# Gate weights split to high and low parts in the first feed-forward, longer reckoned loads, and two token blocks per bank for the sparse queries

## The chip, the cores and the metric

The kernel runs on one core of one Trainium2 chip. The metric is the device time of one execution in microseconds, taken as the median of several runs. The engines are named in the profile as PE (TensorE, matrix products), PEld (its weight loads), DVE (VectorE), ACT (ScalarE), POOL (GpSimd) and SP (SyncE, which issues every DMA here).

## What is computed

One layer on 1024 tokens of width 1024: a first SwiGLU feed-forward (inner width 2816), a mixer, and a second feed-forward, each behind an RMS norm that is scaled and shifted by a conditioning vector. The mixer is what the change is about:

```python
z = h @ w_in
(fq, fk, fv, ff, dq, dk, dv, iq, ik, iw, ga, gb) = jnp.split(z, split_points, axis=-1)
...
ya = fox_attention(fq, fk, fv, log_f).reshape(B, S, FOX_WIDTH)
...
yb = dsa_attention(dq, dk, dv, iq, ik, iw, top_k).reshape(B, S, DSA_WIDTH)
merged = jax.nn.sigmoid(ga) * (ya @ w_br_fox) + jax.nn.sigmoid(gb) * (yb @ w_br_dsa)
return merged @ w_out
```

`ga` and `gb` are the gates, 1024 columns each, so 2048 columns of `w_in`. `dq` are the queries of the sparse attention, 8 heads of 64. The sparse attention keeps for each query the 256 keys with the highest index score, for which the kernel searches a threshold per query.

## The kernel before, in words

**Arithmetic.** Every large product runs as three matmuls (`mm3`, line 457): an operand is held as a high part rounded to the matmul's type and a low part that is the rest, and high x high, high x low and low x high are summed in PSUM. A weight that comes from DRAM is therefore split on the chip: `load_w` (line 565) loads 128x1024 raw values, ScalarE copies them to the high part `wh`, GpSimd subtracts to get the low part `wl`.

**Order of the work.** From line 205 on, the class `Plan` collects the instructions of a stage and puts them into an order for each engine's queue, on a model: `length` (line 302) reckons each instruction, and `flush` (line 322) always places the one that can start first, in rank order among equals. A step marked with `behind = n` gets a rank n instructions later. A DMA on SyncE is reckoned in line 395: it goes over one wire of 345 GB/s that begins 1.3 us after its issue, and its data counts as there 0.7 us after that. GpSimd and VectorE instructions that only touch SBUF are not placed at the same time. What the chip then does in the queues is in that order, at its own pace. A stage's instructions all stand ahead of the next stage's in each queue.

**First feed-forward (to about 690 us).** Eleven pairs of inner blocks go through `up_all` (line 1603), which counts its steps in `k.up_step`, 130 in all: ten for each of the first six pairs, whose first four steps are done before, and fourteen for each of the other five. One step is a product of 12 matmuls. A table `steps` calls further work at given steps; conditioning vectors of later layers are worked in by `extra`. Then `Down` (line 1643) does the second projection. Tiles of 128x512 come from a common pool of 52 (`t512`, line 576), and split weights from 8 pairs of halves.

**The gates' stage (to about 1049 us).** The function `layer` (line 1942) builds one list `g1` (lines 2232 to 2235): the third and fourth group of fox projections, two groups of sparse queries (`dq_group`, line 1026), and between them the 16 gate blocks of the first 512 tokens (`gates`, line 1072). One gate block is 24 matmuls of 512 columns, a tanh on ScalarE and a store of the tile `gt`. Beside it `topk` (line 839) searches the thresholds bit by bit: for three of six query blocks ScalarE counts with Sign (`tks`), for the other three VectorE counts (`tkj`), and small VectorE steps (`tkv`, `tku`, `tkkey`, `tkca`, `tkcand`) set the next bit; at the end `thr` is written. Weights come through `Ahead` (line 1054), which holds three loaded and split blocks ahead, from a ring of five pairs of tiles (`Ring`, line 546).

A group of queries or fox projections in its wide form (`group`, line 963) runs over eight blocks of 128 tokens at once, each in a PSUM bank of its own, taken from `chain8` (line 62): four banks as halves of the two tiles `p2` and four banks `pj`, the same that the gates use. Query blocks are 256 columns, a half bank. When a block is done, ScalarE copies it to the tile `qkv` (`norm_group`, line 1001).

**Attention (to about 1398 us).** Fox attention over four pairs of heads, then sparse attention over four, woven with the masks and the 16 gate blocks of the second 512 tokens (`gates` with PSUM name `py`). Only two split weight blocks are kept here, one ahead. GpSimd scales the probabilities. Then come the branches, the output product and the second feed-forward.

The functions follow, with the line numbers of the profile (all instructions carry L425, the line that issues planned instructions, so tiles tell them apart).

Of the kernel before, what the change touches and what calls it, by code (L numbers as in the profile page):

```python
# [21 lines left out]
D = 1024  # L22
# [3 lines left out]
H = 512  # L26
# [35 lines left out]
def chain8(one, two):  # L62

    while True:
        for _ in range(2):
            t = two()
            yield t[:, 0:H]
            yield t[:, H:T]
        for _ in range(4):
            yield one()  # L70


class Pairs:
# [131 lines left out]
class Plan:  # L205
# [116 lines left out]
    def flush(self, keep=()):  # L322
# [42 lines left out]
        while len(order) < len(tasks):  # L365
# [26 lines left out]
            free[e] = s + d  # L392
            if e == "sync":
                self.wire = max(self.wire, s + 1.3) + t.bytes / 345e3
                end = self.wire + 0.7
                free[e] = max(free[e], self.wire - 5.0)
            t.placed = True
            if t.group:
# [147 lines left out]
class Ring:  # L546
# [12 lines left out]
    def pair(self):  # L559
        p, n = self.split[self.i % len(self.split)]  # L560
        self.i += 1
        return tuple(p.tile([128, D], F32R, tag=t, name=t, bufs=n) for t in ("wh", "wl"))


def load_w(k, src, n):

    nc = k.nc
    raw = k.w.raw()
    nc.sync.dma_start(raw[:, :n], src)
    hi, lo = k.w.pair()  # L570
    nc.scalar.activation(hi[:, :n], raw[:, :n], AF.Copy)
    k.lo_eng.tensor_sub(lo[:, :n], raw[:, :n], hi[:, :n].bitcast(F32))
    return hi, lo
# [389 lines left out]
def group(k, src, n, ptile, wide, done, weight=1.9):  # L963


    if not wide:
        w = load_group(k, src, n)
        for tk in range(8):
            ps = ptile()
            proj_n(k, ps[:, :n], w, n, tk)  # L970
            done(tk, ps)
            tick(k)
            yield
        return
    ps = []
    for i in range(4):
        hi, lo = next(src)
        for tk in range(8):
            if i == 0:
                ps.append(ptile())  # L980
            hf, o = tk // 4, (tk % 4) * 128
            for c in range(2):
                hh, hl = (t[hf][2 * i + c][:, o:o + 128] for t in (k.hh, k.hl))
                cs = slice(c * n, c * n + n)
                mm3(k, ps[tk][:, :n], hh, hl, hi[:, cs], lo[:, cs], i + c == 0, i == 3 and c == 1)
            if i == 3:
                done(tk, ps[tk])
            if tk % 2:
                tick(k)
                yield weight  # L990
# [10 lines left out]
def norm_group(k, p, tmp, src, n, ptile, wide, weight=1.9):  # L1001

    t = [p.tile([128, 4, n], F32, tag="qkv", name="qkv", bufs=3) for _ in range(2)]
    v = tmp.tile([128, 8, 4], F32, tag="fv", name="fv", bufs=2)

    def done(tk, ps):
        k.nc.scalar.activation(t[tk // 4][:, tk % 4, :], ps[:, :n], AF.Copy)
        if tk % 2:
            later(k, 1, lambda: squares(k, tmp, v, t, tk))

    yield from group(k, src, n, ptile, wide, done, weight)
    r = head_factor(k, 32, v.rearrange("p a b -> p (a b)"), tmp, "fn").rearrange("p (a b) -> p a b", a=8)
    for h in range(2):
        x = t[h][:, :, 0:256].rearrange("p a (h d) -> p a h d", h=4)
        k.nc.vector.tensor_mul(x, x, r[:, 4 * h:4 * h + 4, :, None].to_broadcast([128, 4, 4, 64]))
    return t
# [925 lines left out]
def layer(tc, xT, c, pos, ada_w, ada_b, ng, inv, w13a, w2a, w_a, w_f, w_q, w_g, fb, fg, dg, wbr, wout, w13b, w2b, out):  # L1942
    with ExitStack() as es:
# [35 lines left out]
        k.pz_i = 0  # L1979
        k.tails, k.now = [], 0  # L1980
        k.lo_eng = nc.gpsimd
        dram = lambda shape, nm: dp.tile(shape, F32, name=nm)
        d_x = dram([8, 128, T], "d_x")
        d_row = [[dram([1, H], f"d_row{i}{h}") for h in range(2)] for i in range(9)]
        k.d_na = dram([8, 128, NA], "d_na")
# [13 lines left out]
        with ExitStack() as ph:  # L1999
# [24 lines left out]
            def consts():  # L2024
                yield
                nc.vector.tensor_copy(k.ident_r, k.ident)
                nc.vector.tensor_copy(k.ident_b, k.ident)
                cm = t512(k, name="cm")[:, 0:128]
                nc.gpsimd.memset(cm, 0.0)
                nc.gpsimd.affine_select(cm, cm, pattern=[[-1, 128]], compare_op=ALU.is_ge, fill=BIG, base=0,  # L2030
                                        channel_multiplier=1)
                nc.vector.tensor_copy(k.causal_b, cm)
                yield
                nc.vector.tensor_scalar(k.g_dq, k.g_dq, -0.125, None, op0=ALU.mult)
                k.g_fk = g2[:, 1:2]
                nc.vector.tensor_scalar(g2[:, 0:1], g2[:, 0:1], -0.125, None, op0=ALU.mult)
                k.g_fq = g2[:, 0:1]
                yield
                rope_tables(k, pos_i, t512(k, name="rt"), it)
                yield  # L2040

            sq1 = [SquareSum(k, nc.vector), SquareSum(k, nc.vector)]
            wa = []
# [76 lines left out]
            for i in range(2, head):  # L2120
# [3 lines left out]
                if i == 4:  # L2124
# [9 lines left out]
            pos_i = k.c.tile([128, 8], I32, name="pos_i")  # L2134
            nc.sync.dma_start(pos_i, pos)
            more()
            rest = up_all(k, pairs, head, [], {2: [more], 4: [more], 6: [more]}, lambda: down.loads(down.LEAD), chain(consts(), rest),
                          (nc.vector, nc.vector), True, lambda n: n % 2)
            steps = {(5, 4): [lambda: stats(0)]}
            steps.update({(6, c): [lambda c=c: h0(range(c, c + 2))] for c in range(0, 8, 2)})  # L2140
            steps.update({(5, c): steps.get((5, c), []) + [lambda c=c: load_wa(c - 1)] for c in range(1, 9)})
# [4 lines left out]

            for q in range(4 * PAIRS):
                steps.setdefault(divmod(q, PAIRS), []).append(more_mod)
            down.run(steps)
            assert next(rest, None) is None  # L2150
            nc.flush([t for r in down.x for t in r] + [t for r in wa for t in r] + k.hh[0] + k.hl[0] + [a.acc for a in sq1])
            w0s.close()
            w1 = pool(s1, "w1", True, side="right")
# [48 lines left out]
        with ExitStack() as ph:  # L2202
# [14 lines left out]

            parts = []
            for i, (w, n) in enumerate(((w_f[2], 768), (w_f[3], 768), (w_q[0], 512), (w_q[1], 512))):
                parts += [(w[j], n, r5) for j in range(4)] + [(w_g[b], D, r5) for b in range(3 * i, 3 * i + 3)]  # L2220
            ws = Ahead(k, parts + [(w_g[b], D, r5) for b in range(12, 16)] + [(w_g[b], D, r2) for b in range(2)], 3)
            nc.flush(k.hh[0] + k.hl[0] + k.hh[1] + k.hl[1] + [t for w in ws.q for t in w])
        k.ap0 = pool(s3, "att0", True)
        ps = ExitStack()
# [2 lines left out]
        with ExitStack() as ph:  # L2227
            tp = pool(ph, "topk", True)
            pj = lambda: pq.tile([128, H], F32, tag="pj", name="pj", bufs=4)
            bank8 = chain8(pj, p2)  # L2230
            gt = gates(k, ws, 0, tp, pj, 2)
            g1 = chain(fox_group(k, fp, fp, ws, 2, lambda: next(bank8), True), islice(gt, 15),
                       fox_group(k, fp, fp, ws, 3, lambda: next(bank8), True), islice(gt, 15),
                       dq_group(k, fp, fp, tp, ws, 0, lambda: next(bank8), 0.8), islice(gt, 15),
                       dq_group(k, fp, fp, tp, ws, 1, lambda: next(bank8), 0.6), gt)
            beside(behind(nc, topk(k, tp), 100), 66, at(g1, fox_qk(k, 0, None, lambda dt: pj()), (110, 122, 128, 134, 138)), 135.0)
            nc.flush(k.hh[1] + k.hl[1] + k.q2 + k.k2 + [t for w in ws.q for t in w])
        ws.parts, ws.n = [(w_g[b], D, r2) for b in range(2, 16)] + [(wbr[b], D, r2) for b in range(2)], 1
        fox.close()
        s1.close()  # L2240

# [168 lines left out]
```

## Time and profile before

| what | value |
|---|---|
| median of 3 runs | 2230.95 us (2229.25 to 2231.05) |
| profiled execution, its own time | 2230.78 us |
| span of the profiled execution, first to last instruction | 2229.0 us |
| mean granted clock of TensorE | 0.994 |
| TensorE busy | 2166.7 us, 97% |
| VectorE, ScalarE, GpSimd busy | 1638.6, 1145.2, 252.0 us |
| DMA traffic | 315.88 MB, 142 GB/s over the span |

Busy time of an engine is the union of its instructions. Matmuls are pipelined, so a busy TensorE is not one that issues at its peak. An idle time is written behind the instruction that ended it, with the instruction that it waited for. The clock is the share of TensorE's full rate that was granted.

### The profile page before, as it was taken

How to read it: one execution, taken by the hardware profiler on the slowest of the kernel's cores; microseconds unless marked ns; L12 is line 12 of the kernel's file. 1: busy time of each engine (PE TensorE's matmuls, PEld its weight loads, DVE VectorE, ACT ScalarE, POOL GpSimd, SP SyncE). 2: the span in 40 equal slices, each digit the busy share in tenths (PEclk: the TensorE clock that was granted, in tenths of full speed). 3: DMA queues.
4: the chain of work that ended last, by engine and by line, in shares of the span. 5: the costliest groups of instructions: out<-in, count | busy, mean ns of one | idle time of the engine just before them, and what ended most of it. 6: DMA issues, size and time to landing. Idle time of an engine off the chain costs nothing.

```text
span 2229.0 us, 31185 instructions
## 1 busy us (share of the span) xinstructions
PE 2166.7 (97%) x10700; PEld 1782.9 (80%) x10700; DVE 1638.6 (74%) x3095; ACT 1145.2 (51%) x2105; POOL 252.0 (11%) x225
## 2 busy tenths in 40 slices
PE   7999999999999999989999998999999999999999
PEld 5877788887889899977777777777778888888887
DVE  7968776688684698888887677498865755558665
ACT  5634433444464566787777677244443333334443
POOL 0000000000010222223445343000000000000000
PEclk9999999999999999999999999999999999999999
DMA  9245543695421323235232212596224443258520
GB/s 333 95 149 178 173 152 109 213 351 195 125 89 57 109 78 130 96 123 161 90 120 88 72 39 81 202 354 189 66 81 132 137 130 103 96 207 287 166 76 38
DMA packets 186267, 315.88 MB, mean 142 GB/s; under 512 B 27238, under 2 KB 51814, under 8 KB 186108
## 3 DMA queue, kind: packets, MB, share of 16 engines
q1 hardware_dynamic: 186108, 313.89, 42.4%
q8 instruction: 84, 1.38, 0.3%
q14 instruction: 75, 0.61, 0.1%
HBM read 237.53 MB, written 76.28 MB: 141 GB/s over the span
## 4 chain that ended last, share of the span: by engine, by line
PE 82%; DVE 8%; ACT 5%; DMA 3%; issue 2%; SPq 0%; POOL 0%; DVEq 0%; ACTq 0%; POOLq 0%
PE bs L425 34%; PE b L425 28%; PE py L425 7%; PE pj L425 6%; PE p L425 5%; PE pt L425 2%; DVE qkv L425 1%; ACT tks L425 1%; DVE xc L425 1%; DMA mraw<-in_ada_w 1%; DMA wr<-in_w_f 1%; ACT pth L425 1%; ACT pr L425 1%; ACT wh L425 1%; DVE wl L425 1%
## 5 line engine op out<-in xcount | busy, mean ns | idle before, releaser
L425 PE MATMUL bs<-h,wh 128*128 128x512 f32 x1728 | 543.0, 395 | 1.6 <-ACT bs L425 1.3
L425 ACT ACTIVATE wh<-wr 128x512 fp32r<-128x512 f32 (+2 forms) x366 | 246.5, 679 | 451.7 <-PE bs L425 208.3
L425 PEld LDWEIGHTS bs<-h,wh 128*128 128x128 f32 x1728 | 322.9, 188 | 81.9 <-ACT bs L425 5.7
L425 PE MATMUL b<-h,wh 128*128 128x512 f32 x1088 | 344.8, 397 | 5.7 <-ACT z L425 2.6
L425 PE MATMUL bs<-h,wl 128*128 128x512 f32 x864 | 338.7, 393 | 0.5 <-DVE wl L425 0.5
L425 DVE TENSOR_TENSOR wl<-wr,wh 128x512 fp32r<-128x512 f32 x308 | 205.4, 686 | 123.5 <-ACT wh L425 116.6
L425 PEld LDWEIGHTS b<-h,wh 128*128 128x128 f32 x1088 | 205.0, 189 | 55.5 <-ACT z L425 3.5
L425 PE MATMUL b<-h,wl 128*128 128x512 f32 x544 | 214.7, 395 | 0.1
L425 PEld LDWEIGHTS bs<-h,wl 128*128 128x128 f32 x864 | 162.2, 188 | 39.2 <-DVE wl L425 0.9
L425 ACT ACTIVATE wh<-a 128x512 fp32r<-128x512 f32 x132 | 83.3, 631 | 174.4 <-PE b L425 93.0
L425 POOL TENSOR_TENSOR wl<-wr,wh 128x1024 fp32r<-128x1024 f32 (+2 forms) x58 | 123.8, 2137 | 328.6 <-ACT wh L425 323.3
L425 DVE TENSOR_TENSOR wl<-a,wh 128x512 fp32r<-128x512 f32 x132 | 91.3, 692 | 88.1 <-ACT wh L425 83.5
L425 PE MATMUL b<-wh 128*128 128x512 f32 x352 | 137.2, 390 | 0.7 <-ACT mrow L425 0.7
L425 PE MATMUL b<-wh,wl 128*128 128x512 f32 x352 | 137.0, 389 | 0.0
L425 PE MATMUL b<-wl,wh 128*128 128x512 f32 x352 | 137.0, 389 | 0.0
L425 PE MATMUL pj<-wh,h 128*128 128x384 f32 (+1 forms) x512 | 125.8, 324 | 0.3 <-ACT wh L425 0.2
L425 PEld LDWEIGHTS b<-h,wl 128*128 128x128 f32 x544 | 102.8, 189 | 25.1 <-DVE wl L425 0.7
L425 DVE TENSOR_TENSOR z<-bs,z 128x512 f32<-128x512 f32 x116 | 79.3, 687 | 58.7 <-PE bs L425 36.8
L425 POOL TENSOR_SCALAR pr<-pr,mn 128x128 f32<-128x128 f32 (+7 forms) x128 | 100.0, 801 | 134.7 <-DVE mn L425 127.5
L425 DVE TENSOR_TENSOR wl<-g,wh 128x512 fp32r<-128x512 f32 x154 | 106.5, 694 | 2.5 <-ACT wh L425 2.5
L425 ACT ACTIVATE pr<-pr,mn 128x256 f32<-128x256 f32 (+7 forms) x128 | 98.4, 770 | 18.0 <-DVE mn L425 17.7
L425 PE MATMUL bs<-wl,wh 128*128 128x512 f32 x264 | 103.1, 391 | 2.1 <-DVE wl L425 1.9
(322 smaller groups left out, 4405.2 us busy)
## 6 DMA issues: line engine op xcount, KB each, us to landing
d_g<-z SPq DMA_DIRECT2D x154, 256.0 KB, 2.1
g<-d_g SPq DMA_DIRECT2D x154, 256.0 KB, 4.7
mraw<-in_ada_w SPq DMA_DIRECT2D x144, 256.0 KB, 5.3
wr<-in_w13a SPq DMA_DIRECT2D x112, 256.0 KB, 5.3
wr<-in_w13b SPq DMA_DIRECT2D x88, 256.0 KB, 4.6
wr<-in_w_g SPq DMA_DIRECT2D x32, 512.0 KB, 4.2
a<-in_w2a SPq DMA_DIRECT2D x44, 256.0 KB, 5.1
a<-in_w2b SPq DMA_DIRECT2D x44, 256.0 KB, 5.3
```

The costliest lines, as they stand in the source:

```text
L425: getattr(getattr(self.tc.nc, e), t.op)(*map(real, t.a), **{n: real(v) for n, v in t.kw.items()})
```

## The change

The weights of the 16 gate blocks are split once, during the first feed-forward, into DRAM tensors `d_wg` of high and low parts; 64 calls of a generator, from step 30 to step 124, do two halves of 512 columns per block (a load, a ScalarE copy, a GpSimd subtraction, then two stores), ranked 200 instructions behind. Both later passes over the gates load the parts straight into the tiles `wh` and `wl`, two DMAs of 512 KB in place of a load, a copy and a subtraction. Split tiles of the ring are handed out in order. The plan reckons that a DMA's data is there 1.0 us later than before. In the groups of sparse queries two token blocks of 256 columns share a bank, so that a group takes the four half tiles of `p2` alone and one ScalarE copy empties two blocks; the fox groups (384 columns) keep one block per bank.

```diff
@@ Plan.flush @@
-                end = self.wire + 0.7
+                end = self.wire + 1.7
@@ Ring.pair @@
-        return tuple(p.tile([128, D], F32R, tag=t, name=t, bufs=n) for t in ("wh", "wl"))
+        return tuple(p.tile([128, D], F32R, tag=t, name=t, bufs=n, in_turn=True) for t in ("wh", "wl"))
@@ load_w @@
+    if isinstance(src, tuple):
+        t = k.w.pair()
+        for part, d in zip(t, src):
+            nc.sync.dma_start(part[:, :n].bitcast(F32), d)
+        return t
@@ group, wide @@
-    ps = []
+    ps, m = [], H // n
...
-            if i == 0:
+            if i == 0 and tk % m == 0:
                 ps.append(ptile())
...
-                mm3(k, ps[tk][:, :n], hh, hl, hi[:, cs], lo[:, cs], i + c == 0, i == 3 and c == 1)
-            if i == 3:
-                done(tk, ps[tk])
+                mm3(k, ps[tk // m][:, tk % m * n:tk % m * n + n], hh, hl, hi[:, cs], lo[:, cs], i + c == 0,
+                    i == 3 and c == 1, tk % m > 0)
+            if i == 3 and tk % m == m - 1:
+                done(tk, ps[tk // m])
@@ norm_group @@
-        k.nc.scalar.activation(t[tk // 4][:, tk % 4, :], ps[:, :n], AF.Copy)
+        m = H // n if wide else 1
+        k.nc.scalar.activation(t[tk // 4][:, tk % 4 - m + 1:tk % 4 + 1, :], ps[:, :m * n].rearrange("p (a b) -> p a b", a=m),
+                               AF.Copy)
@@ layer @@
+        d_wg = split_in(16, D, "wg")
...
+        todo = [(w[i], d[i]) for w, d in (((w_g, d_wg),)) for i in range(len(d))]
...
+            def parts():
+
+                for src, dst in todo:
+                    n = dst[0].shape[1]
+                    m = n if n <= H else n // 2
+                    for c in range(0, n, m):
+                        nc.behind = 200
+                        t, hi, lo = (t512(k, dt, "gw")[:, :m] for dt in (F32, F32R, F32R))
+                        nc.sync.dma_start(t, src[:, c:c + m])
+                        nc.scalar.activation(hi, t, AF.Copy)
+                        nc.gpsimd.tensor_sub(lo, t, hi.bitcast(F32))
+                        nc.behind = 0
+                        yield
+                        nc.behind = 200
+                        for d, x in zip(dst, (hi, lo)):
+                            nc.sync.dma_start(d[:, c:c + m], x.bitcast(F32))
+                        nc.behind = 0
+                        yield
...
+            gw = parts()
+            steps = {2: [more], 4: [more], 6: [more]}
+            for n in range(64):
+                steps.setdefault(30 + 96 * n // 64, []).append(lambda: next(gw, None))
...
-                parts += [(w[j], n, r5) for j in range(4)] + [(w_g[b], D, r5) for b in range(3 * i, 3 * i + 3)]
-            ws = Ahead(k, parts + [(w_g[b], D, r5) for b in range(12, 16)] + [(w_g[b], D, r2) for b in range(2)], 3)
+                parts += [(w[j], n, r5) for j in range(4)] + [(d_wg[b], D, r5) for b in range(3 * i, 3 * i + 3)]
+            ws = Ahead(k, parts + [(d_wg[b], D, r5) for b in range(12, 16)] + [(d_wg[b], D, r2) for b in range(2)], 3)
...
-                       dq_group(k, fp, fp, tp, ws, 0, lambda: next(bank8), 0.8), islice(gt, 15),
-                       dq_group(k, fp, fp, tp, ws, 1, lambda: next(bank8), 0.6), gt)
+                       dq_group(k, fp, fp, tp, ws, 0, lambda: next(bank4), 0.8), islice(gt, 15),
+                       dq_group(k, fp, fp, tp, ws, 1, lambda: next(bank4), 0.6), gt)
...
-        ws.parts, ws.n = [(w_g[b], D, r2) for b in range(2, 16)] + [(wbr[b], D, r2) for b in range(2)], 1
+        ws.parts, ws.n = [(d_wg[b], D, r2) for b in range(2, 16)] + [(wbr[b], D, r2) for b in range(2)], 1
```

`chain4` yields the two halves of `p2` tiles in turn. Smaller lines without effect on the work (empty loops, unused tensors) are left out.

## Rows read from the trace of the kernel before

**Rows 1.** The page, part 1: busy us of each engine.
```profile
PE 2166.7 (97%) x10700; PEld 1782.9 (80%) x10700; DVE 1638.6 (74%) x3095; ACT 1145.2 (51%) x2105; POOL 252.0 (11%) x225
```

**Rows 2.** Stretches: length; busy us of PE, PEld, DVE, ACT, POOL; clock, DMA, GB/s.
```profile
192.00:457.00 265.00, 264.71 (x1139) 212.25 (x1139) 188.38 (x299) 102.29 (x177) 0.00 (x0) 1.00 0.54 179
457.00:506.00 49.00, 48.32 (x213) 39.27 (x212) 43.57 (x72) 23.95 (x43) 0.00 (x0) 1.00 0.99 356
```

**Rows 3.** The same columns: the gates' stage, and the attention.
```profile
843.00:1049.00 206.00, 197.08 (x1102) 175.37 (x1100) 170.05 (x505) 161.66 (x297) 58.67 (x30) 0.98 0.39 124
1049.00:1398.00 349.00, 332.77 (x2302) 266.06 (x2303) 269.14 (x599) 250.93 (x548) 149.41 (x155) 0.98 0.27 85
```

**Rows 4.** The same columns, in stretches of 50 us.
```profile
600.00:650.00 50.00, 50.00 (x226) 41.52 (x225) 34.28 (x59) 26.80 (x49) 10.95 (x8) 1.00 0.27 85
...
950.00:1000.00 50.00, 45.43 (x274) 40.90 (x275) 42.84 (x128) 41.11 (x80) 13.68 (x8) 0.93 0.42 132
```

**Rows 5.** Timeline of PE: start us, us, instruction, idle before.
```profile
1037.79 0.39 PE L425 MATMUL pj<-h,wl 128*128 128x512 f32 x1
...
1049.16 1.06 PE L425 MATMUL pt<-ident,nat 128*128 128x128 f32 x8 [1.29 <-DMA nat<-d_qkv]
```

**Rows 6.** Timeline of DVE at the end of the threshold search.
```profile
1042.10 0.17 DVE L425 TENSOR_SCALAR tkca<-tkkey 128x3 f32<-128x3 f32 x1
...
1046.06 0.17 DVE L425 SCALAR_TENSOR_TENSOR tkkey<-tkv,tkkey 128x3 f32<-128x3 f32 x1
...
1049.21 0.16 DVE L425 TENSOR_TENSOR thr<-tkku,tkm 128x3 uint32<-128x3 uint32 x1
```

**Rows 7.** The tile tks: ns min/median/max, first and last start us.
```profile
L425 ACT ACTIVATE tks<-tkh,tkca x51: 921/1042/1159, 843.5 to 948.9; 128x1024 bf16<-128x1024 uint16 x17, 128x896 bf16<-128x896 uint16 x17, 128x768 bf16<-128x768 uint16 x17
...
L425 ACT ACTIVATION_READ_ACCUMULATOR tks<-tkl,tkca x48: 185/188/240, 953.5 to 1045.6; 128x1 f32 x48
```

**Rows 8.** Groups by form, 843 to 1049 us: busy us, mean ns, idle before.
```profile
L425 POOL TENSOR_TENSOR wl<-wr,wh 128x1024 fp32r<-128x1024 f32 x16 | 38.5, 2404 | 95.0 <-ACT wh L425 95.0
L425 POOL TENSOR_TENSOR wl<-wr,wh 128x512 fp32r<-128x512 f32 x8 | 10.3, 1292 | 45.3 <-ACT wh L425 45.3
...
L425 ACT ACTIVATE wh<-wr 128x1024 fp32r<-128x1024 f32 x16 | 16.9, 1054 | 10.9 <-issue 10.9
```

**Rows 9.** Groups by form of DVE, 843 to 1049 us.
```profile
L425 DVE TENSOR_TENSOR qkv<-qkv,fnr 128x1024 f32<-128x1024 f32 x9 | 14.9, 1690 | 0.1
L425 DVE TENSOR_TENSOR tku<-tkcnt,tklim 128x3 uint32<-128x3 f32 x32 | 11.7, 365 | 0.8
L425 DVE TENSOR_TENSOR tkv<-tksgn,tklim 128x3 f32<-128x3 f32 x32 | 11.4, 355 | 23.4 <-ACT tks L425 23.2
...
L425 DVE SCALAR_TENSOR_TENSOR tkkey<-tkv,tkkey 128x3 f32<-128x3 f32 x32 | 5.2, 162 | 1.1
L425 DVE TENSOR_TENSOR qkv<-qkv,g_dq 128x1024 f32<-128x1024 f32 x4 | 4.9, 1216 | 0.0
```

**Rows 10.** Timeline of PE around the sparse queries.
```profile
949.07 0.50 PE L425 MATMUL p<-wh,h 128*128 128x256 f32 x2 [1.05 <-ACT qkv L425]
951.05 0.51 PE L425 MATMUL p<-wh,h 128*128 128x256 f32 x2 [1.48 <-ACT qkv L425]
...
995.58 0.72 PE L425 MATMUL pj<-h,wh 128*128 128x512 f32 x2 [3.52 <-ACT qkv L425]
```

**Rows 11.** Groups by form of ACT in the attention, 1049 to 1400 us.
```profile
L425 ACT ACTIVATE wh<-wr 128x1024 fp32r<-128x1024 f32 x16 | 17.0, 1060 | 4.1 <-PE py L425 4.1
```

**Rows 12.** The chain that ended last: start us, us, what.
```profile
473.45 49.95 PE b L425 x219
```

**Rows 13.** Groups by form of POOL, whole span.
```profile
L425 POOL TENSOR_TENSOR wa<-war,wa 128x432 fp32r<-128x432 f32 x8 | 11.0, 1374 | 480.2 <-DVE wl L425 461.2 <-DMA g<-d_g 6.9 <-DVE nacc L425 6.4
```

**Rows 14.** The page, part 6: DMA issues, KB each, median us to landing.
```profile
wr<-in_w_g SPq DMA_DIRECT2D x32, 512.0 KB, 4.2
```

**Rows 15.** Waits of PE, whole span: us in total, times, longest.
```profile
PE bs L425 <- ACT wh L425: 2.8, 1, 2.8
```

More of the change, by code (lines that the diff above doesn't have):

```diff
@@ L70, in chain8, with chain4 @@
             yield one()
+def chain4(two):
+    while True:
+        t = two()
+        yield t[:, 0:H]
+        yield t[:, H:T]
 class Pairs:
@@ L1981, in layer @@
         k.lo_eng = nc.gpsimd
-        dram = lambda shape, nm: dp.tile(shape, F32, name=nm)
+        dram = lambda shape, nm, dt=F32: dp.tile(shape, dt, name=nm)
+        split_in = lambda n, m, nm: [tuple(dram([128, m], f"d_{nm}{i}{x}") for x in "hl") for i in range(n)]
+        d_wg = split_in(16, D, "wg")
+        d_wf = [split_in(4, 768, f"wf{i}") for i in range(4)]
+        d_wq = [split_in(4, 512, f"wq{i}") for i in range(2)]
+        todo = [(w[i], d[i]) for w, d in (((w_g, d_wg),)) for i in range(len(d))]
         d_x = dram([8, 128, T], "d_x")
@@ L2136, in layer @@
             more()
-            rest = up_all(k, pairs, head, [], {2: [more], 4: [more], 6: [more]}, lambda: down.loads(down.LEAD), chain(consts(), rest),
+            gw = parts()
+            steps = {2: [more], 4: [more], 6: [more]}
+            for n in range(64):
+                steps.setdefault(30 + 96 * n // 64, []).append(lambda: next(gw, None))
+            rest = up_all(k, pairs, head, [], steps, lambda: down.loads(down.LEAD), chain(consts(), rest),
                           (nc.vector, nc.vector), True, lambda n: n % 2)
+            assert next(gw, 0) == 0
             steps = {(5, 4): [lambda: stats(0)]}
@@ L2148, in layer @@
                 steps.setdefault(divmod(q, PAIRS), []).append(more_mod)
+            for q in range(0, 0):
+                steps.setdefault(divmod(q, PAIRS), []).append(lambda: next(gw, None))
             down.run(steps)
-            assert next(rest, None) is None
+            assert next(rest, None) is None and next(gw, 0) == 0
             nc.flush([t for r in down.x for t in r] + [t for r in wa for t in r] + k.hh[0] + k.hl[0] + [a.acc for a in sq1])
@@ L2230, in layer @@
             bank8 = chain8(pj, p2)
+            bank4 = chain4(p2)
             gt = gates(k, ws, 0, tp, pj, 2)
```

## The prediction

> **What bounds the kernel now.** The page comes first: TensorE is busy for 2166.7 of 2229.0 us [rows 1], so the most that any change without fewer matmuls can win is the 62 us in which it stands still, what it loses at its lower clock, and small waits inside the attention. The table of stretches shows where. In the two feed-forwards TensorE stands still for almost nothing: 264.71 of 265 us busy from 192 to 457 us, with VectorE at 188.38, ScalarE at 102.29 and GpSimd at nothing [rows 2]. From 843 to 1049 us it loses 8.9 us, and 16.2 us in the attention from 1049 to 1398 us [rows 3]. From 950 to 1000 us the mean granted clock is 0.93 [rows 4]; the lower of its two levels is 1.2 GHz, half of 2.4, so the clock takes another 3.5 us of these 50.
>
> What ends the stage of the gates is read last, from two timelines. TensorE's last gate matmul of the first token half starts at 1037.79 us; it then takes gate blocks of the second half as filler, until it stands still 1.29 us before 1049.16 [rows 5]. VectorE's timeline says why: the last sparse threshold is written at 1049.21 us, and the attention's VectorE work stands behind it in the same queue [rows 6]. So the search for the thresholds, a chain of 33 rounds of ScalarE signs and VectorE updates, sets when attention starts. One round with nothing in its way takes from 1042.10 to 1046.06, 4.0 us [rows 6]; the 33 run from 843.5 to 1045.6 us [rows 7], 6.1 us each. About 70 us of that chain is other work.
>
> **Term 1, the gates' stage: -17 us.** Sixteen gate blocks lose their split here: 16 GpSimd subtractions (2.404 us each, 38.5 us) and 16 ScalarE copies (1.054 us each, 16.9 us) [rows 8]. VectorE pays for the subtractions: the 128x3 updates tku and tkv take 365 and 355 ns on average, an equal one that seldom meets one takes 162, and the multiplication of qkv takes 1690 against 1216 [rows 9]. That is 32 x 0.203 + 32 x 0.193 + 9 x 0.474 = 17.0 us of standing. The same groups hold the 512-wide subtractions of other weights, 10.3 us against 38.5 [rows 8], and smaller groups that I leave out stand too; I let the two cancel. The chain can therefore lose at most 17.0 + 16.9 = 34 us. It loses nothing if all of it falls where the chain waits anyway: VectorE already idles 23.2 us for the signs [rows 9]. With no row to choose by, I take the middle, 17 us: thresholds at 1032 instead of 1049 us.
>
> This needs TensorE to be done by then. It stands at 949.07, 951.05 and 995.58 us for 1.05, 1.48 and 3.52 us, each time for ScalarE to empty a bank of the sparse queries, and runs the next matmuls at the lower clock [rows 10]. With two token blocks per bank the query groups keep to four banks of their own, so the gate block behind a group needs none of them: 6.05 us of standing and the 3.5 us of clock go, and the last gate ends near 1028, not 1038 us. Attention can then start 17 us sooner, and at most 21. Without this part it would be 11. Eight evacuations instead of sixteen save ScalarE some 2 us, hidden in the same middle.
>
> **Term 2, filler: +4 us.** Some 10 us of second-half gate matmuls run before 1048 us now. With TensorE free from 1028 and attention from 1032, about 7 us of them move into the attention. Their cost lies between 0 (TensorE has 16.2 us of standing there [rows 3]) and 7; I take 4, as each of those gaps is short.
>
> **Term 3, attention: -4 us.** Fourteen of its sixteen 1.060 us copies on ScalarE go [rows 11], 14.8 us out of 250.93 busy in 349 [rows 3], and 14 x 2.4 = 34 us of GpSimd, which also scales the probabilities. No engine is full there, so the gain lies between 0 and 15 and I take it small, as it shortens only steps that happened to wait behind a split.
>
> **Term 4, the first feed-forward: +2 us.** Thirty-two half blocks come in, from step 30 of 130 to step 124: at 2.8 us a step (12 matmuls at 233 ns, 192 to 457 us holding 1139 [rows 2]), and the down projection's first long run of matmuls begins at 473.45 us [rows 12], so this is 192 to 457 us. ScalarE gets 32 copies of half width, about 0.6 us each by the 1.054 of a full one, 19 us on 102.29 in 265, hidden. GpSimd gets 32 x 1.292 = 41.3 us [rows 8], with nothing in its queue. VectorE has 76.6 us free [rows 2] to absorb the standing. SyncE gets 32 loads and 64 stores of 256 KB, 25.2 MB: 95 GB/s more on 179, under the 356 seen [rows 2]. Stores that wait for GpSimd hold up weight loads queued behind them by a subtraction's length, while a pair's weights are asked for a pair, 28 to 39 us, ahead. The nearest row for the whole is the eight subtractions of the narrow weights, 1374 ns each [rows 13], all eight inside a stretch where TensorE is busy for 50.00 of 50 us [rows 4]. Bounds 0 and 41; I take 2, near that row.
> The Trainium skill, SBUF — State Buffer, "Who interferes with whom", says that a VectorE instruction with two SBUF inputs and a GpSimd one that reads SBUF shut each other out for a whole instruction. By it most of the work moved here meets such instructions; the trace agrees where tku and qkv stretch [rows 9].
>
> **Edits at nothing.** The gates' loads become two of 512 KB per block, 4.2 us to land [rows 14], asked for three blocks of at least 5.6 us ahead, one block in the attention, where 16 blocks are spread over 349 us, some 20 us apart; they now wait on SyncE for TensorE to finish with the tiles, with stores of gates behind them. If that lead were gone, each block would cost about 6 us. Splits handed out in turn follow the order that the blocks have anyhow. **The longer reckoning of loads** reorders every planned stage. It can win the waits of TensorE that hang on loads (2.8 us [rows 15] and the 1.29 us at 1049 [rows 5]) and can make as many: -4 to +4, I take 0.
>
> **Sum.** -17 + 4 - 4 + 2 = -15. The profiled execution took 2230.78 us (span 2229.0 and 1.78 around it); the median, 2230.95, is 0.17 above it. 2230.78 - 15 gives 2216 us. A measurement of this kernel tells about 0.2%, 4.5 us, from no change.
>
> **Rivals.**
> *The forecast*, 0.60, its own range 2207 to 2226.
> *The start of attention doesn't carry to the end*, 0.18. The chain keeps its length because ScalarE's and VectorE's other work fills the freed slots, or attention, at 77% VectorE and 72% ScalarE [rows 3], takes its time back with the displaced filler. For it: the search has a lower rank than the main work in the schedule. Against it: the VectorE standing is gone whatever the order. Terms 1 to 3 shrink to some -4, time 2229.
> *VectorE and GpSimd block each other in the first feed-forward*, 0.10, the slower side. VectorE is 71% busy from 192 to 457 us, so of 41.3 us of GpSimd some 29 meet VectorE at work; from 457 to 506 us it is 89% busy (43.57 of 49) with DMA at 0.99 [rows 2], and splits placed late, because the common pool of 52 tiles has too few free, would land there. If all 29 reached TensorE instead of 2, the time is 2243; it is slower than before once 17 us do. Against it: TensorE's weights are split up to eight halves ahead, and [rows 4]. By that section of the Trainium skill this is the outcome wherever VectorE has no slack.
> *More comes free*, 0.12: thresholds at TensorE's floor (-21), filler absorbed (+2), ScalarE's relief felt in full (-12), the feed-forward unharmed: -31, time 2200.
>
> **How the numbers follow.** Faster by over 0.2% (under 2226.5): nearly all of the forecast, 0.58, all of the last rival and a little of the first, 0.04: 0.74. Slower (above 2235.4): 0.10 and 0.02 of the first rival: 0.12. The rest, 0.14, is the same. The range takes the forecast, the second case and the nearer part of the last, 2202 to 2234, and leaves out the lock.
>
> **What would show it.** Right: thr written near 1032 with tku and tkv near 162 ns; no standing for qkv before the gates; TensorE as busy from 192 to 506 as now; GpSimd with 32 subtractions of 1.3 us there. Wrong: a chain of unchanged length, TensorE waiting for wl or z before 506 us, or an attention longer than 349 us by what its start gained.

## The result, and the profile after

The changed kernel takes 2219.85 us, median of 4 runs (2216.98 to 2220.44), beside 2230.67 us (2229.25 to 2231.05, 4 runs) of the kernel before: a ratio of 0.995, interval 0.9933 to 0.9967. That is 10.8 us faster where 15 were forecast; the forecast range of 2202 to 2234 us holds it. The profiled execution took 2220.0 us, its span is 2218.3.

The page of the kernel after, part 1 (as [rows 1]), and one line of part 6, the new loads of the gates' weights (as [rows 14]):

```profile
PE 2164.5 (98%) x10700; PEld 1780.1 (80%) x10700; DVE 1637.0 (74%) x3095; ACT 1132.3 (51%) x2097; POOL 221.9 (10%) x225
...
gw<-in_w_g SPq DMA_DIRECT2D x32, 256.0 KB, 4.2
```

The stretches of [rows 2, 3] in the kernel after (same columns):

```profile
192.00:457.00 265.00, 264.51 (x1138) 211.81 (x1137) 205.51 (x294) 116.01 (x207) 43.27 (x30) 1.00 0.77 257
457.00:506.00 49.00, 48.32 (x212) 39.07 (x211) 40.70 (x67) 24.88 (x45) 2.82 (x2) 1.00 1.03 370
843.00:1049.00 206.00, 202.09 (x1153) 180.97 (x1152) 154.22 (x513) 146.44 (x278) 22.92 (x18) 1.00 0.52 175
1049.00:1398.00 349.00, 336.56 (x2328) 269.31 (x2327) 270.54 (x590) 240.79 (x533) 114.68 (x137) 1.00 0.36 114
```

The work has moved as the change says. GpSimd has 43.27 us in the first feed-forward, where it had none, 35.8 us less in the gates' stage and 34.7 less in the attention; TensorE's busy time in the feed-forward is the same within 0.2 us. In the gates' stage TensorE stands still 3.9 of 206 us (8.9 before), in the attention 12.4 of 349 (16.2 before).

The groups of VectorE in the kernel after, 835 to 1043 us, the stretch of its search (as [rows 9]):

```profile
L433 DVE TENSOR_TENSOR qkv<-qkv,fnr 128x1024 f32<-128x1024 f32 x10 | 11.9, 1222 | 0.1
...
L433 DVE TENSOR_TENSOR tku<-tkcnt,tklim 128x3 uint32<-128x3 f32 x32 | 7.1, 223 | 0.7
...
L433 DVE TENSOR_TENSOR tkv<-tksgn,tklim 128x3 f32<-128x3 f32 x32 | 6.2, 193 | 17.7 <-ACT tks L433 17.6
```

The stretched instructions are short again: 223 and 193 ns for 365 and 355, 1222 for 1690. Yet the thresholds hardly gain. Tiles `tks` and `thr` of the kernel after (as [rows 6, 7]):

```profile
L433 ACT ACTIVATE tks<-tkh,tkca x51: 921/1042/1151, 839.9 to 943.0; 128x1024 bf16<-128x1024 uint16 x17, 128x896 bf16<-128x896 uint16 x17, 128x768 bf16<-128x768 uint16 x17
...
L433 DVE TENSOR_TENSOR thr<-tkku,tkm x1: 164/164/164, 1042.4 to 1042.4; 128x3 uint32<-128x3 uint32 x1
```

From the first sign to the last threshold, called **the search** from here on, 202.5 us go by, against 205.7 before (843.5 to 1049.2). Some 14 us of standing are gone (32 x 0.142 + 32 x 0.162 + 9 x 0.468), and the search is 3.2 us shorter. So two things want an explanation: why the search keeps its length, and where 10.8 us come from all the same.

The table shows where the time went in every kernel run. Its columns are differences to the kernel before, in us of one profiled execution each, between four marks of TensorE's work: the last narrow matmul (`bs<-wa`, 723.4 us before), the last gate matmul of the first half (1038.2), the last output matmul of the attention (`py`, 1402.9) and the end of the span (2229.0). The search is given by its own length. Several kernels have one plan in the first column (after, no_bank, reckon_first, reckon_att and the two first_keep) and differ there by up to 2.6 us; reckon_first and reckon_att have one plan in the second and differ by 3.9. So only larger differences are read.

| kernel | to 723.4 | index scores and gates | attention | rest | sum | search |
|---|---|---|---|---|---|---|
| after | 0.8 | -3.6 | -8.4 | 0.3 | -10.8 | 202.5 |
| no_split | -2.2 | -0.6 | -7.4 | -1.4 | -11.6 | 206.3 |
| no_bank | 0.9 | -3.5 | -8.8 | 0.0 | -11.4 | 196.5 |
| no_reckon | 8.9 | -8.0 | -8.7 | -0.9 | -8.7 | 187.5 |
| only_split | 9.8 | -6.3 | -7.8 | -1.9 | -6.2 | 187.7 |
| only_reckon | -0.8 | -0.3 | -6.3 | -1.3 | -8.7 | 206.8 |
| only_bank | 2.1 | 1.5 | -0.2 | 1.1 | 4.5 | 211.7 |
| reckon_first | -1.5 | -6.6 | -7.4 | -0.5 | -15.9 | 187.4 |
| turn_late | 0.6 | -3.3 | -9.1 | 0.4 | -11.5 | 202.5 |
| first_keep_act | -1.7 | -9.7 | -7.6 | -2.7 | -21.7 | 199.6 |
| first_keep_pool | 0.3 | 0.7 | 4.5 | -0.3 | 5.2 | 214.1 |
| split_dve | 5.8 | -7.4 | -9.7 | -1.8 | -13.2 | 187.8 |
| reckon_att | -1.0 | -10.5 | -8.7 | 0.6 | -19.6 | 187.4 |

### The profile page after: what moved, and what is told of

Read it like the earlier page. It is cut to its first block, busy times and chain, and to the rows that moved or that the text cites. A ratio compares the mean times of both kernels' runs of the same rounds, so it can differ in the third digit from the quotient of the medians.

```text
span 2218.3 us, 31445 instructions
## 1 busy us (share of the span) xinstructions
PE 2164.5 (98%) x10700; PEld 1780.1 (80%) x10700; DVE 1637.0 (74%) x3095; ACT 1132.3 (51%) x2097; POOL 221.9 (10%) x225
## 4 chain that ended last, share of the span: by engine, by line
PE 85%; DVE 6%; ACT 3%; DMA 3%; issue 2%; SPq 1%; POOL 0%; DVEq 0%; ACTq 0%
PE bs L433 34%; PE b L433 27%; PE pj L433 7%; PE py L433 7%; PE p L433 7%; PE pt L433 3%; DVE macc L433 1%; DMA mraw<-in_ada_w 1%; DVE s L433 1%; DVE xc L433 1%; ACT pr L433 1%; ACT pth L433 1%; SPq L433 1%; DVE xb L433 1%; DVE wl L433 0%
## 5 line engine op out<-in xcount | busy, mean ns | idle before, releaser
L433 ACT ACTIVATE wh<-wr 128x512 fp32r<-128x512 f32 (+2 forms) x334 | 212.0, 642 | 389.5 <-PE bs L433 183.9
L433 PE MATMUL bs<-wh,wl 128*128 128x512 f32 x264 | 102.5, 389 | 0.0
L433 PE MATMUL pj<-wh,h 128*128 128x384 f32 x384 | 102.4, 338 | 0.0
```

The lines of the kernel that those rows point to most:

```text
L433: getattr(getattr(self.tc.nc, e), t.op)(*map(real, t.a), **{n: real(v) for n, v in t.kw.items()})
```

## The experiments

The theory to be tried was the prediction's: the split of the gates' weights wins the time, by taking GpSimd's subtractions away from VectorE's search. The rivals: the longer reckoning wins it, or the shared banks do.

**no_split**: the change without the split; the gates' weights are loaded raw and split where they are used, as before.

```diff
-        todo = [(w[i], d[i]) for w, d in (((w_g, d_wg),)) for i in range(len(d))]
+        todo = [(w[i], d[i]) for w, d in () for i in range(len(d))]
...
-        ws.parts, ws.n = [(d_wg[b], D, r2) for b in range(2, 16)] + [(wbr[b], D, r2) for b in range(2)], 1
+        ws.parts, ws.n = [(w_g[b], D, r2) for b in range(2, 16)] + [(wbr[b], D, r2) for b in range(2)], 1
```

> The change without its first part: the gates' weights are loaded raw and split where they are used, as before; the longer reckoning, the splits in turn and the shared banks stay. Theory (the split out of the gates' stage and the attention carries the gain): 2226 to 2234 us, no better than before by more than 5. Rival (the shared banks carry it, since they take away TensorE's standing for qkv): 2219 to 2223, as the whole change.

Measured: 2221.04 us (8 runs), ratio 0.9957 (0.9941 to 0.9972). The theory falls as it stood: without the split the gain is nearly the same. The search is as long as before, 206.3 us, and the attention is 7.4 us shorter all the same. The time is the one that the rival named, but its reason, the shared banks, falls with only_bank below.

**no_reckon**: the change with the old reckoning.

```diff
-                end = self.wire + 1.7
+                end = self.wire + 0.7
```

> The change with loads reckoned as before (0.7 in place of 1.7). Theory (the longer reckoning costs: the head runs 1.7 us late before any gate work, and the index scores end with a stall at the lower clock that puts the gates' stage 4 us back): both go, 2212 to 2217 us. Rival (the longer reckoning is part of the gain, as the queues then fit the loads): 2222 or more.

Measured: 2224.54 us (12 runs), 0.9972 (0.996 to 0.9984). The rival holds, not the theory. The split works without the longer reckoning, and the search is even shorter, 187.5 us. But the first feed-forward now loses 8.9 us. The longer constant is the nearer one there: a load of `gw` lands 4.2 us after its issue (the line of part 6 above), and for 256 KB on a free wire the planner reckons 2.8 us with the old constant (1.3, 0.76 on the wire, 0.7) and 3.8 with the new.

**only_split**: the old reckoning and one token block per bank, so that the split alone is left (the edits of no_reckon and of the next one together).

> Kernel of before plus the split in the first feed-forward alone (with splits in turn, without the longer reckoning and the shared banks). Theory: most of the gain, 2217 to 2223 us; first feed-forward not more than 1 us longer up to the last narrow matmul. Rival (the split is only paid for by the other two parts): 2228 or more.

Measured: 2223.89 us (12 runs), 0.997 (0.9958 to 0.9983). The split alone wins 6 us, just less than the theory's range, and its first feed-forward loses 9.8 us where the theory allowed 1; the search is 18.0 us shorter. The timeline of TensorE in only_split, 238 to 302 us (idle before and its cause in brackets), shows a part of that loss:

```profile
240.94 0.73 PE L433 MATMUL bs<-h,wh 128*128 128x512 f32 x2 [0.95 <-DVE z L433]
266.62 0.73 PE L433 MATMUL bs<-h,wh 128*128 128x512 f32 x2 [2.19 <-DVE z L433]
301.40 0.74 PE L433 MATMUL bs<-h,wh 128*128 128x512 f32 x2 [2.08 <-DVE z L433]
```

What came before the wait that ends at 266.62 stands in the timelines of VectorE and GpSimd of the same kernel:

```profile
257.56 0.75 DVE L433 SCALAR_TENSOR_TENSOR macc<-mraw,cond,macc 128x512 f32<-128x512 f32 x1
...
262.50 3.46 DVE L433 SCALAR_TENSOR_TENSOR macc<-mraw,cond,macc 128x512 f32<-128x512 f32 x2
265.88 2.80 DVE L433 TENSOR_TENSOR z<-bs,z 128x512 f32<-128x512 f32 x4
...
260.86 4.56 POOL L433 TENSOR_TENSOR gw<-gw 128x512 fp32r<-128x512 f32 x2 [10.02 <-DMA gw<-in_w_g]
```

An `macc` of 0.75 us takes 3.46 for two while GpSimd subtracts, and the two subtractions take 4.56 us, where one alone takes 1.29 [rows 8]. GpSimd had stood idle for 10.02 us until the load. Only then comes the `z` that TensorE waits for. The waits of TensorE for `z` from 150 to 740 us, in the kernel before and in only_split (us in all, times, longest):

```profile
PE bs L425 <- DVE z L425: 0.3, 1, 0.3
```

```profile
PE bs L433 <- DVE z L433: 5.4, 4, 2.2
```

These 5.1 us more are about half of the 9.8. TensorE's standing up to the last narrow matmul grows by 5.6 us in all (18.7 to 24.3); the rest is busy time, 704.7 to 708.9 us, which no run divides further.

**no_bank**: the change with one token block of sparse queries per bank.

```diff
-    ps, m = [], H // n
+    ps, m = [], 1
...
-        m = H // n if wide else 1
+        m = 1
...
-                       dq_group(k, fp, fp, tp, ws, 0, lambda: next(bank4), 0.8), islice(gt, 15),
-                       dq_group(k, fp, fp, tp, ws, 1, lambda: next(bank4), 0.6), gt)
+                       dq_group(k, fp, fp, tp, ws, 0, lambda: next(bank8), 0.8), islice(gt, 15),
+                       dq_group(k, fp, fp, tp, ws, 1, lambda: next(bank8), 0.6), gt)
```

> The change with one token block per bank again for the sparse queries. Theory: some 4 us of the gain go, 2222 to 2226 us, with TensorE standing for qkv ahead of gate blocks by 1 to 4 us again. Rival (the banks carry the gain): 2228 or more. If the split alone sets the start of attention, nothing changes: 2219 to 2221.

Measured: 2216.53 us (6 runs), 0.9935 (0.9917 to 0.9953). The time is below all three that were expected: the shared banks are not needed.

**only_bank**: the shared banks added to the kernel before, the edit of no_bank the other way round.

> Kernel of before with two token blocks of sparse queries per bank and nothing else. New theory: TensorE's standing for qkv near 950 and 992 us shrinks, the end moves by 0 to 5 us, 2226 to 2231. Rival (the banks carry the run without the split): 2219 to 2223.

Measured: 2233.12 us (12 runs), 1.0012 (1.0002 to 1.0021): alone they cost 2 us, where 0 to 5 were to be won. The standing of TensorE that they were to remove does not shrink. Its waits for `qkv` from 843 to 1049 us (us in all, times, longest), in the kernel before, then in only_bank, then in only_split, which has no shared banks, then in the kernel after:

```profile
PE p L425 <- ACT qkv L425: 4.3, 5, 1.5
PE pj L425 <- ACT qkv L425: 3.5, 1, 3.5
```

```profile
PE p L433 <- ACT qkv L433: 8.7, 6, 3.5
```

```profile
PE pj L433 <- ACT qkv L433: 1.6, 1, 1.6
PE p L433 <- ACT qkv L433: 1.1, 2, 0.6
```

```profile
PE p L433 <- ACT qkv L433: 3.9, 6, 0.7
```

The split takes most of this standing away, 7.8 us to 2.7, with the banks as they were. The longer reckoning alone takes away some of it too (4.9 us are left in only_reckon).

**only_reckon**: the kernel before with the longer reckoning alone (the edit of no_reckon, the other way round).

> Kernel of before with one number changed: a DMA's data reckoned 1.7 us after the wire in place of 0.7. New theory (the reckoning alone orders the queues so that the gates' stage and the attention lose less, and the split adds little to it): 2217 to 2222 us. Rival (the run without the split owed its gain to the shared banks): 2228 to 2232.

Measured: 2222.31 us (7 runs), 0.9967 (0.9955 to 0.998). One constant of the planner wins 8.7 us, 6.3 of it in the attention, with a search of 206.8 us. So the split alone wins some 6 us and the reckoning alone some 9, and together 10.8: part of both is the same gain.

Where that common part lies, the attention shows, from TensorE's last gate matmul of the first half to its last output matmul (columns as in [rows 3]); first the kernel before, then after, then only_reckon, then no_split:

```profile
1038.20:1402.90 364.70, 347.35 (x2377) 277.83 (x2378) 277.69 (x620) 260.10 (x565) 154.33 (x158) 0.98 0.30 92
```

```profile
1035.50:1391.90 356.40, 343.96 (x2377) 275.48 (x2378) 269.81 (x610) 245.53 (x547) 118.87 (x143) 1.00 0.37 118
```

```profile
1037.10:1395.50 358.40, 344.32 (x2378) 277.01 (x2378) 275.63 (x615) 260.38 (x565) 153.49 (x158) 0.99 0.30 94
```

```profile
1035.40:1392.80 357.40, 342.58 (x2378) 274.24 (x2378) 275.50 (x619) 260.10 (x567) 153.76 (x158) 1.00 0.30 94
```

The work is the same, 2377 or 2378 matmuls. TensorE stands still for 17.4 us before and 12.4 after, and is busy for 347.4 and 344.0: of the gain 4.9 us are standing and 3.4 busy time. In only_reckon the two shares are 3.3 and 3.0 us, in no_split 2.5 and 4.8. The busy time is longest where the granted clock is lowest, 0.98 before and 0.99 or 1.00 in the others. The larger part of the clock's loss lies at the start of the attention, in the same order of kernels:

```profile
1030.00:1080.00 50.00, 44.76 (x265) 35.05 (x264) 41.43 (x115) 38.32 (x80) 21.31 (x19) 0.90 0.41 133
```

```profile
1030.00:1080.00 50.00, 46.50 (x305) 37.07 (x304) 33.65 (x99) 36.72 (x84) 16.95 (x21) 0.97 0.60 198
```

```profile
1030.00:1080.00 50.00, 44.98 (x279) 35.97 (x278) 41.60 (x109) 40.11 (x84) 24.21 (x23) 0.93 0.46 145
```

```profile
1030.00:1080.00 50.00, 44.32 (x296) 34.97 (x296) 42.45 (x119) 40.46 (x90) 24.97 (x23) 1.00 0.51 165
```

In the kernel before TensorE stands still there for 5.2 of 50 us at a granted clock of 0.90; in no_split it stands 5.7 us and keeps the full clock. So in these rows the length of the standing alone does not decide the clock. How the standing falls may, and any new plan shuffles that; which order keeps the clock was not tried by itself.

**reckon_first**: the change with the longer reckoning up to the narrow weights alone (`nc.land` is read where 1.7 stood) and the old one from the index scores on.

```diff
+        self.land = 1.7
...
-                end = self.wire + 1.7
+                end = self.wire + self.land
...
+        nc.land = 0.7
```

> The change with the longer reckoning in the first feed-forward's plan alone, 0.7 behind it. Theory (the longer reckoning pays for the split in the first feed-forward, where the run with 0.7 lost 9 us, and behind it the split pays by itself): first feed-forward within 2 us of before at its last narrow matmul, thresholds 15 us or more earlier than before, 2212 to 2216 us. Rival (the reckoning is needed in the gates' stage and the attention too): 2220 or more.

Measured: 2213.31 us (5 runs), 0.9927 (0.9913 to 0.9941). The longer reckoning is what saves the feed-forward (-1.5 us there for 8.9 with the old one), and what spoils the search behind it (187.4 us for 202.5). How it does, the timelines of the kernel after show, first of VectorE, then of ScalarE:

```profile
857.18 0.69 DVE L433 TENSOR_REDUCE fv<-fsq 128x8 f32<-128x512 f32 x1 [9.92 <-ACT fsq L433]
...
954.00 0.69 DVE L433 TENSOR_REDUCE fv<-fsq 128x8 f32<-128x512 f32 x1 [3.67 <-ACT fsq L433]
...
852.10 0.85 ACT L433 ACTIVATE wh<-wr 128x768 fp32r<-128x768 f32 x1 [8.72 <-issue]
```

The plan has put a sum of squares `fv` ahead of the next rounds of the search in VectorE's queue. ScalarE stands still ahead of the copy of a weight ("issue": the profile shows nothing that it waits for), its squares come late, and the search waits behind `fv`. The waits of VectorE for `fsq` from 838 to 1060 us, in the kernel after and in reckon_first:

```profile
DVE fv L433 <- ACT fsq L433: 19.4, 6, 9.9
```

```profile
DVE fv L434 <- ACT fsq L434: 2.9, 3, 2.0
```

This wait is 16.5 us longer in the kernel after, and its search 15.1. The two do not go one to one: in no_bank the wait is 16.0 us and the search 196.5, only 9.1 longer than in reckon_first. Neither the split nor the reckoning does it alone: 2.2 us in only_reckon, 2.6 in only_split, 2.0 in no_split.

**turn_late**: the change with split tiles handed out in turn only from the gates' stage on. The index scores took 2.6 us longer in the kernel after, and the turn could be the reason.

```diff
-        return tuple(p.tile([128, D], F32R, tag=t, name=t, bufs=n, in_turn=True) for t in ("wh", "wl"))
+        return tuple(p.tile([128, D], F32R, tag=t, name=t, bufs=n, in_turn=self.turn) for t in ("wh", "wl"))
```

> The change with splits handed out in turn only from the gates' stage on. In all four runs with splits in turn the stretch from the last narrow matmul to the first gate blocks grew by 3 to 6 us. Theory (the turn causes that): 2215 to 2217 us. Rival (the order of loads causes it, whatever the turn): 2219 to 2221.

Measured: 2217.32 us (5 runs), 0.9945 (0.9932 to 0.9959). The time lies just outside both ranges, but the stretch of the index scores is as long as in the kernel after, the search too, to the tenth. The turn is not the cause. Nor is it clear that there is a loss to explain: the index scores take 101.3 us in the kernel after and 98.8 before, but 97.7 in first_keep_pool and 103.3 in reckon_first, whose plans are the same there.

**first_keep_act** and **first_keep_pool** divide the relief of the gates' stage between ScalarE and GpSimd. On top of reckon_first, a gate block loads its raw weights and one part, and one engine still works: in the first ScalarE copies the high part and GpSimd does nothing; in the second the high part is loaded and GpSimd subtracts. The first edit below is shown against reckon_first, the second against the first; the lists of blocks, which now hand over the raw weights too, are left out.

```diff
-        for part, d in zip(t, src):
-            nc.sync.dma_start(part[:, :n].bitcast(F32), d)
-        return t
+        raw = k.w.raw()
+        nc.sync.dma_start(raw[:, :n], src[0])
+        hi, lo = k.w.pair()
+        nc.sync.dma_start(lo[:, :n].bitcast(F32), src[2])
+        nc.scalar.activation(hi[:, :n], raw[:, :n], AF.Copy)
+        return hi, lo
```

```diff
-        nc.sync.dma_start(lo[:, :n].bitcast(F32), src[2])
-        nc.scalar.activation(hi[:, :n], raw[:, :n], AF.Copy)
+        nc.sync.dma_start(hi[:, :n].bitcast(F32), src[1])
+        k.lo_eng.tensor_sub(lo[:, :n], raw[:, :n], hi[:, :n].bitcast(F32))
```

> The run with the longer reckoning in the first feed-forward alone, but a gate block loads its raw weights and its low part, and ScalarE copies the high part as before: GpSimd's subtraction is gone, ScalarE's copy is back. Theory (the chain of thresholds was lengthened by VectorE standing behind GpSimd): thresholds still 12 to 19 us earlier than before. Rival (ScalarE's copies between the signs lengthened it): 0 to 8 us earlier.

> The mirror of it: a gate block loads its raw weights and its high part, and GpSimd subtracts the low part as before; ScalarE's copy is gone. Theory (VectorE behind GpSimd): thresholds 0 to 8 us earlier than before, tku and tkv near 350 ns on average again. Rival (ScalarE's copies): 12 to 19 us earlier.

Measured, one execution each: 2209.24 us with ScalarE's copies, 2235.95 with GpSimd's subtractions (2228.72 the median of the kernel before). With the copies the last threshold comes 11.6 us earlier than before, just short of the theory's 12; with the subtractions it comes 7.8 us later, which neither side expected. The groups of VectorE from 843 to 1049 us, with ScalarE's copies and then with GpSimd's subtractions:

```profile
L434 DVE TENSOR_TENSOR tkv<-tksgn,tklim 128x3 f32<-128x3 f32 x32 | 6.6, 206 | 27.4 <-ACT tks L434 27.2
L434 DVE TENSOR_TENSOR tku<-tkcnt,tklim 128x3 uint32<-128x3 f32 x31 | 5.9, 192 | 0.8
```

```profile
L434 DVE TENSOR_TENSOR tkv<-tksgn,tklim 128x3 f32<-128x3 f32 x31 | 14.8, 477 | 21.0 <-ACT tks L434 21.0
L434 DVE TENSOR_TENSOR tku<-tkcnt,tklim 128x3 uint32<-128x3 f32 x32 | 12.2, 381 | 0.7
```

What the split wins by itself hangs on GpSimd's subtractions, not on ScalarE's copies: with them the attention loses 4.5 us, without them it wins 7.6. ScalarE's copies do lengthen the search by 12 us over reckon_first, GpSimd's subtractions by 27, and in the kernel before, where both are at work, it is only 18 longer: the costs do not add, so the order that each plan makes counts too. TensorE does not notice the longer search of the first: its scores and gates win 9.7 us against reckon_first's 6.6, which is no less. These two executions have no interval, and 26.7 us lie between them.

**split_dve**: only_split, with the 32 subtractions of the first feed-forward on VectorE, to part the blocking from the late loads.

```diff
-                        nc.gpsimd.tensor_sub(lo, t, hi.bitcast(F32))
+                        nc.vector.tensor_sub(lo, t, hi.bitcast(F32))
```

> The split alone with the short reckoning, its 32 subtractions in the first feed-forward on VectorE in place of GpSimd. With GpSimd the last narrow matmul came 9 us late. Theory (VectorE stood behind GpSimd subtractions that ran at the wrong moment, and z came late): 0 to 4 us late. Rival (loads that land later than reckoned hold VectorE up by themselves): 7 us late or more.

Measured, one execution: 2217.63 us. The feed-forward loses 5.8 us where GpSimd's subtractions lost 9.8 (8.9 in no_reckon, on the same plan). That falls between what the two theories wanted. TensorE's waits for `z` from 150 to 740 us, 5.4 us in only_split, are

```profile
PE bs L433 <- DVE z L433: 1.7, 3, 0.7
```

So some 4 us are the blocking, and the rest stays when no GpSimd instruction runs beside the feed-forward's products (none from 160 to 520 us). VectorE has 32 subtractions more to do there, which can hold it up as well. The loads are the likely cause (VectorE waits 20.1 us for `in_w13a` from 160 to 520 us in only_split, 14.3 before, 8.8 after), but no run parted them further.

**reckon_att**: reckon_first with the longer reckoning once more from the attention on (`nc.land = 1.7` ahead of its pool), to see whether the gains of the stages add.

> The run with the longer reckoning in the first feed-forward alone, with the longer reckoning in the attention and behind it too, so that only the index scores and the gates' stage are planned with 0.7. Theory (the gains of attention under the two reckonings lie in different parts of it and add): 2208 to 2212 us. Rival (attention is bound by TensorE's arrival, and gives 9 to 10 us either way): 2213 to 2215.

Measured: 2211.26 us (6 runs), 0.992 (0.9907 to 0.9933). It is the fastest of the kernels with an interval, 17.5 us under the 2228.72 of the kernel before in the same comparison; between the two ratios, 0.992 and 0.995, it is 7 us better than the change as made, and the intervals just meet. The time is the one that the theory named. Its attention wins 8.7 us and reckon_first's 7.4, which is within what two executions differ by; that the stages' gains do not eat each other is what it shows, not that its last edit is worth something.

## Why the prediction was right, and where its steps were not

The time, the sign and the range came out, but not by the terms: a gain forecast for the gates' stage stayed away, and one that was not reckoned with came in the attention. That the sum landed near is luck.

**Term 1, the gates' stage, -17: right for the split, wrong for the change.** The split by itself shortens the search by 18.0 us (205.7 to 187.7, and 187.4 to 187.8 in all five kernels with the whole split and the old reckoning in that stage), near the 17 that were taken as the middle of 0 to 34 with no row to choose by. VectorE's standing behind GpSimd, the working behind it, is there: the stretched groups give up some 14 of the 17.0 us, and come back in first_keep_pool. ScalarE's copies cost the search too. What failed is the value for the longer reckoning of loads, "-4 to +4, I take 0": it gives 15 of the 18 back by an order that lets the search wait for `fsq`. In the change the last threshold comes 6.8 us earlier, not 17, and TensorE's last gate matmul 2.7, not 10.

**That the thresholds set the attention's start failed as well.** [rows 5] itself names a load for the 1.29 us, and TensorE goes on at 1049.16 us, ahead of the last threshold at 1049.21 [rows 6]. The last thresholds of no_split and of only_split (as [rows 7]):

```profile
L433 DVE TENSOR_TENSOR thr<-tkku,tkm x1: 163/163/163, 1047.2 to 1047.2; 128x3 uint32<-128x3 uint32 x1
```

```profile
L433 DVE TENSOR_TENSOR thr<-tkku,tkm x1: 163/163/163, 1040.0 to 1040.0; 128x3 uint32<-128x3 uint32 x1
```

In no_split it comes 11.8 us behind TensorE's last gate matmul (1035.4), as before (11.0); in only_split 1.7 us ahead of it (1041.7). From that matmul on, the attention is 7.4 and 7.8 us shorter, nearly alike. In only_bank and first_keep_pool the last threshold comes 17 to 18 us behind, and the attention wins nothing; whether a threshold that late costs, no run shows by itself.

**The step on the banks failed too.** "6.05 us of standing and the 3.5 us of clock go" was put down to the shared banks. Alone they leave 8.7 us of waits for `qkv` where there were 7.8, and cost 2 us; the change leaves 3.9 with them and 3.8 without (no_bank), and is no slower without; the split alone leaves 2.7 us. So TensorE's bound hung on what else the engines did. ScalarE, which empties the banks, runs the search's signs and the copies of the weights too; that this is why is likely, and was not tried by itself.

**Terms 2 and 3, filler +4 and attention -4: 0 together, and it was -4 to -8.** Counted from the last threshold, as the terms are, the attention takes 349.5 us in the change and 353.7 before; counted from the last gate matmul, 8.4 less. The working asked how much ScalarE and GpSimd are relieved. no_split relieves neither and wins 7.4 us there, so that is not what the gain needs: 4.9 us of the 8.4 are TensorE's standing and the rest goes with its clock, which was not priced in the attention. Its lower level cost 5.0 us of the 50 from 1030 us (0.10 of 50), and costs 1.5 in the kernel after. The split wins this without the reckoning and the reckoning without the split, so it is counted once.

**Term 4, the first feed-forward, +2 of 0 to 41: right in the sum (+0.8), by an accident.** With the old reckoning the split costs 8.9 to 9.8 us there, so the nearest row, the eight narrow subtractions [rows 13], was too kind. A likely reason is that its stretch moved 85 GB/s [rows 4], where 192 to 457 us moves 257 in the kernel after. The rival in which VectorE and GpSimd block each other was thus a real one, with its sign that TensorE waits for `z` (5.4 us); the longer reckoning, priced at nothing, is what kept it away. The section "Who interferes with whom" of the Trainium skill's SBUF — State Buffer describes this shutting out, and only_split agrees with it (3.46 us for two `macc` of 0.75).

**The longer reckoning, 0 within -4 to +4: the term that was mis-sized most.** Alone it is -8.7 us. It is not one effect but three: -8 to -11 in the feed-forward once the split is there (8.9 to 0.8, 9.8 to -1.5), +15 on the search with the split, -6 to -7 in the attention, which the split wins as well. The bounds came from waits of TensorE that were put down to loads (2.8 and 1.29 us), and reordering all planned stages is not bounded by these.

The rival in which the start of the attention does not carry to the end was half right: the search did keep its length. But its reason (other work in the freed slots) and its consequence (2229 us) were not what came; the end moved without the thresholds.

## What to carry to other kernels

A constant of a planner that reorders every stage has to be tried alone and stage by stage: here it saved one stage and spoilt the next, and using it only where it helps is worth some 5 to 7 us by the medians, with intervals that overlap the change's or just meet it. A chain that starts a stage is worth its length only until the next bound, so the stage's end has to be priced from both sides. Work moved from a crowded stage into a quiet one on the same pair of engines keeps its blocking, and here it hid only where the plan reckoned with loads that land late enough.

## What the runs showed of the hardware

The lower clock at the start of the attention costs as much as the waits around it: 5.0 us beside 5.2 us of standing from 1030 to 1080 us in the kernel before. A group of 12 matmuls of 64x384 took 2.92 us there, at a granted clock of 0.50; in only_reckon a like group, behind a wait as long, took 1.81 at the full clock (timelines of TensorE, each with the stretch of the group, columns as in [rows 3]):

```profile
1051.09 2.92 PE L425 MATMUL p<-qs 64*128 64x384 f32 x12 [0.86 <-DVE mn L425]
...
1051.09:1054.01 2.92, 2.92 (x13) 2.21 (x14) 2.12 (x8) 2.92 (x9) 1.42 (x4) 0.50 1.02 340
```

```profile
1050.03 1.81 PE L433 MATMUL p<-qs 64*128 64x384 f32 x12 [0.95 <-DVE mn L433]
...
1050.03:1051.84 1.81, 1.81 (x14) 1.28 (x15) 1.38 (x7) 1.81 (x7) 0.30 (x1) 1.00 1.02 380
```

Blocking goes both ways: two of GpSimd's 128x512 subtractions took 4.56 us beside VectorE's `macc` in only_split, against 1.29 for one [rows 8]. All 32 of them there, from 150 to 520 us, took 1623 ns on average:

```profile
L433 POOL TENSOR_TENSOR gw<-gw 128x512 fp32r<-128x512 f32 x32 | 51.9, 1623 | 259.0 <-ACT gw L433 184.4 <-DMA gw<-in_w_g 37.2 <-DMA g<-d_g 14.0
```

So a subtraction moved beside a busy VectorE lengthens itself too.
